# Where column sums, squares of x and one weight slot stand in a two-layer decoder kernel

## The chip, the cores and the metric

The kernel runs on one core of a Trainium2 chip. A core has a matrix engine (TensorE, PE in the profile; its weight loads are listed apart as PEld), a vector engine (VectorE, DVE), a scalar engine (ScalarE, ACT), a general engine (GpSimd, POOL) and an engine that only issues transfers (SyncE, SP). They share one on-chip memory of 128 partitions (SBUF); products land in a second one (PSUM) of eight banks, and transfers (DMA) bring data from main memory. Every engine works through its own list of instructions in order and waits for the others by semaphores. The metric is the device time of one execution in microseconds.

## What is computed

The reference is a decoder of two layers on 256 tokens of width 1024, each of which also attends into a fixed memory of 256 rows. Everything is float32. Cut to what matters here:

```
def _rmsnorm(x, g):
    y = x * lax.rsqrt(jnp.mean(x * x, axis=-1, keepdims=True) + EPS)
    return y * g

def _sq_relu_mlp(h, w_up, w_down):
    u = jax.nn.relu(h @ w_up)
    return (u * u) @ w_down

# layer A
h = _rmsnorm(x, a_norm_attn);  z = h @ a_w_in          # q, k, v, qm
...                                                    # rotation of q and k, differential attention
kv = _rmsnorm(mem, a_mem_norm) @ a_w_mem_kv            # keys and values of the memory
x = x + concat(o_self, o_mem) @ a_w_out
x = x + _sq_relu_mlp(_rmsnorm(x, a_norm_mlp), a_w_up, a_w_down)
# layer B: the same frame, block attention, with kv_norm, b_norm_attn, b_mem_norm, b_norm_mlp
# at the end: _rmsnorm(x, final_norm)
```

The norm's factor of a token, 1/sqrt(mean of squares), can be applied behind a product, since it scales whole rows. So the products run on `x * gain`, and the factor is needed only where a result leaves PSUM.

## The kernel before

**Products in three passes.** Every float32 operand is split in a high part (a rounded copy, `wh` for weights) and a low part (the rest, `wl`). A product is high times high, high times low and low times high. The weights come in 192 chunks of 128 x 1024 (512 KB each) into a ring `w` of four slots; ACT makes `wh` (line 354, a copy that rounds), DVE makes `wl` (line 356, a subtraction with two inputs), each into a ring of six slots. A slot is taken as the lowest free one when its first user is placed. `x` is kept transposed in `xT` (eight tiles of 128 x 256), and `x * gain` is split in the same way into `xn` (lines 370 and 372).

**Two places for xn.** `xn` lies in one room that is `LEAD` = 16 elements (64 bytes) longer than its content. The up stages read it from the room's start (`xnt`), the other stages 64 bytes further (`xnn`). The weights' slots all have one place within a line of 512 bytes, the same as that of `xnn`, by the order in which the tiles are laid out.

**A planner writes the order.** The program first lists its steps (`P.add`): engine, a duration in ns from a formula, what is read and written, and a priority, which is the step's number less a shift (`P.shift`). `Plan.order` then plays the steps through on its own clock: an engine that is free takes the ready step of the lowest priority whose buffers are free. The instructions of each engine are issued in the order that results. Transfers are steps of an engine `dma` whose durations are bytes over a rate: 390 bytes per ns for large ones, 290 for small ones, 310 for those of the start, and 1900 ns more until they land (3000 for `xnat`). A step of POOL and a step of DVE with two inputs are kept apart in time. No duration of the planner is measured when the kernel runs; if the chip is later than the plan, an engine waits at the instruction that the plan put next.

**Stages.** From 0 to about 124 us runs the attention of layer A (`mixer_a`), to 212 the up products of its MLP, to 282 the down products, to 410 the attention of layer B, to 500 the up products and to the end the down products of layer B. The first block of `mixer_a` (`qk_block`, products at lines 515 and 520) uses the first four weight chunks; its results leave PSUM scaled with x's factors (`ropes`, line 551), are rotated by POOL (line 562) and DVE (lines 568 and 570) and are turned by PE (line 586) for the first attention scores. There is one `ropes` buffer, so the two halves of the tokens follow each other. Then comes the product of the memory's rows (`mem_a`), whose tiles are made from `memt` by `mem_tiles`.

**Three ways to a norm's factor** (class `Stats`):
- `whole` loads the rows themselves (`xnat` or `mnat`, two transfers of 512 KB), squares and sums them along the row on ACT (line 456, four instructions) and ends with some twelve small DVE instructions (lines 461 to 464, with lines 412 to 421).
- `add` squares a tile of `xT` on ACT (line 473) and adds it to `sqa` on POOL (line 474).
- `rstd` sums `sqa` over the partitions with two one-column products on PE (line 483), which need a PSUM bank of the class `t`, and ends with the same chain on DVE, or with two instructions if only the square is wanted.

Layer A's first norm and the memory's norm use `whole`: `ra.whole(xnat, 2, 3000, pri=119.5)` and `mr.whole(mnat, 3)`.

**Up stages** (`mlp_up`). Sixteen steps `b` of two chunks each. A chunk is 16 products with `wh` and 8 with `wl`, all of 256 columns: a slice of weights is stationary and `xnt` moves (line 848). Between `b` = 4 and 11 the tiles of `xT` go through `add`; at `b` = 14 the column sum, `st.rstd(True)`, is listed, two steps (four chunks) ahead of the stage's end. Its result is used when the down stage's sums are scaled.

**Down stages** (`natural_down`, products of 512 columns at line 898) open four PSUM banks of the class `t`, and take part of the weights in pairs of chunks through `fast_pair`, where seven products replace eight.

Of the kernel before, what the change touches and what calls it, by code (L numbers as in the profile page):

```python
# [10 lines left out]
F32R = mybir.dt.float32r  # L11
# [6 lines left out]
D, S, FF = 1024, 256, 4096  # L18
KT = D // 128
# [6 lines left out]
FAST = (1, 3, 5, 7, 9, 11)  # L26
CW = 1024
LEAD = 16
WARM = 34


# [179 lines left out]
def t_act(n, psum=False, scale=False):  # L211
    return (51 if psum else 93) + 0.835 * n + (93 if scale else 0)


def t_dve(n, scalar=False):
    return 69 + 1.041 * n + (61 if scalar else 0)
# [11 lines left out]
def tile_hybrid(ctx: ExitStack, tc: tile.TileContext, x0, xa, xb, xc, memt, xnat, mnat, w0, wall, consts, fgain, out):  # L228
    nc = tc.nc
    const = ctx.enter_context(tc.tile_pool(name="const", bufs=1))  # L230
    ring = ctx.enter_context(tc.tile_pool(name="ring", bufs=1))
# [7 lines left out]
    P = Plan(caps, ("acc", "w", "wh", "wl", "v") + tuple(f"B{i}" for i in range(8)))  # L239
    uid = [0]  # L240

    def name(s):
        uid[0] += 1
        return f"{s}_{uid[0]}"

    def buf(cls, shape, dt=F32, pool=None):
        pool = pool or ring
        return Buf(cls, lambda slot: pool.tile(shape, dt, name=name(cls), tag=f"{cls}{slot}", bufs=1))
# [25 lines left out]
    NG = len(GAINS) * KT  # L274
    xg = fixed([128, NG + KT * S], "xT")
    xT = xg[:, NG:].rearrange("p (k s) -> p k s", k=KT)
    xroom = fixed([128, KT * 2 * S + LEAD], "xn", F32R)
    xnt, xnn = [xroom[:, a:a + KT * 2 * S].rearrange("p (k a s) -> p k a s", k=KT, a=2) for a in (0, LEAD)]
    g = {n: xg[:, i * KT:(i + 1) * KT] for i, n in enumerate(GAINS)}
# [18 lines left out]
    wu = psum.tile([128, 512], F32, name="wu", tag="t0", bufs=1)  # L298
    for _ in range(WARM):
        nc.tensor.matmul(wu[:, 0:128], ones_b, ones_b, start=True, stop=True)  # L300
# [22 lines left out]
        return deco  # L323

    def dma(dst, src, nbytes, r=(), w=(), pri=None, rate=0, lag=1900):
        rate = rate or (290 if nbytes <= 2100 * 128 else 390)
        P.add(("dma", max(470, nbytes / rate), lambda: nc.sync.dma_start(dst(), src)), r, w, lag=lag, pri=pri)  # L327


    st_ = {"i": 0, "pieces": 2, "layer": "A"}  # L330

    def chunk(dma_pieces=1, **a):
        i = st_["i"]
        st_["i"] += 1
        w = buf("w", [128, CW])
        h = buf("wh", [128, CW], F32R)
        l = buf("wl", [128, CW], F32R)
        hs = (0, 1)
        if dma_pieces == 1:
            dma(lambda: w.t, wall[i], 4 * 128 * CW, w=[(w, 0), (w, 1)], **a)  # L340
        else:
            for p in hs:
                dma(lambda p=p: w.t[:, p * 512:(p + 1) * 512], wall[i][:, p * 512:(p + 1) * 512] if i else w0[p],
                    256 * CW, w=[(w, p)], pri=(2 * i + 0.5 * p - 0.5) if i else 4 * p - 6, **a)
        old, P.shift = P.shift, EARLY["w" + st_["layer"]]
        for p in (hs if st_["pieces"] == 2 else [hs]):
            q = p if isinstance(p, tuple) else (p,)
            sl = slice(q[0] * 512, q[-1] * 512 + 512)
            n = 512 * len(q)
            if i == 0 and q[0] == 0:  # L350
                P.add(("dve", t_dve(n), lambda sl=sl: nc.vector.tensor_copy(h.t[:, sl], w.t[:, sl])),
                      [(w, x) for x in q], [(h, x) for x in q], pri=-9)
            else:
                P.add(("act", t_act(n), lambda sl=sl: nc.scalar.copy(h.t[:, sl], w.t[:, sl])),  # L354
                      [(w, x) for x in q], [(h, x) for x in q])
            P.add(("dve", t_dve(n), lambda sl=sl: nc.vector.tensor_sub(l.t[:, sl], w.t[:, sl],  # L356
                                                                       h.t[:, sl].bitcast(F32))),
                  [(w, x) for x in q] + [(h, x) for x in q], [(l, x) for x in q], port=True)
        P.shift = old
        return h, l  # L360
# [18 lines left out]
    def big(i, shape, dt=F32):  # L379
        return buf(f"B{i}", shape, dt)  # L380
# [12 lines left out]
    def mem_tiles(gname):  # L393

        hs, ls = [], []
        T = Tiles(lambda k: hs[k // 4].t[:, k % 4], lambda k: ls[k // 4].t[:, k % 4],
                  lambda k: (hs[k // 4], k % 4), lambda k: (ls[k // 4], k % 4))
        for a in range(2):
            w = buf("w", [128, 4, S])
            hs.append(buf("wh", [128, 4, S], F32R))  # L400
            ls.append(buf("wl", [128, 4, S], F32R))
            dma(lambda w=w: w.t, memt[:, 4 * a:4 * a + 4], 4 * 128 * CW, w=[w])
            for i in range(4):
                k = 4 * a + i
                early("mem")(split_scaled)(lambda w=w, i=i: w.t[:, i], [w], g[gname][:, k:k + 1], T, k)
        return T
# [396 lines left out]
    def mlp_up(st, sums=()):  # L803

        us = [big(i, [128, 4, 2, S], F32R) for i in range(8)]
        st_["pieces"] = 1
        for b in range(16):
            if 4 <= b < 12:
                st.add(lambda m=b - 4: xT[:, m], [("x", b - 4)])
            if b == 14:  # L810
                st.rstd(True)
            u = buf("u", [128, 2, S])
            ps = bank("acc")
            for mi in range(2):
                wh, wl = chunk()
                up_chunk(ps, mi, wh, wl)
            k0 = 2 * b % 4
            P.add(("act", t_act(512, True), lambda u=u, ps=ps: nc.scalar.activation(
                u.t, ps.t.rearrange("p (a s) -> p a s", a=2), AF.Relu)), [ps], [u])
            P.add(("act", t_act(512), lambda u=u: nc.scalar.activation(u.t, u.t, AF.Square)), [u], [u])  # L820
            if b in sums:
                dst, keys = sums[b]

                def blocks(u=u, dst=dst):
                    a = [u.t[:, k, hf * 128:hf * 128 + 128] for hf in range(2) for k in range(2)]
                    s = [dst()[:, i * 128:i * 128 + 128] for i in range(4)]
                    nc.vector.tensor_add(s[0], a[2], a[3])
                    nc.vector.tensor_sub(s[1], s[0], a[0])
                    nc.vector.tensor_sub(s[2], a[0], a[2])
                    nc.vector.tensor_sub(s[3], a[1], s[1])  # L830
                P.add(("dve", 4 * t_dve(128) + 100, blocks), [u], keys, port=True)
            P.add(("act", t_act(512), lambda u=u, t=us[b // 2], k0=k0: nc.scalar.copy(t.t[:, k0:k0 + 2, 0], u.t)),  # L832
                  [u], [(us[b // 2], b)])
            P.add(("dve", t_dve(512), lambda u=u, t=us[b // 2], k0=k0: nc.vector.tensor_sub(  # L834
                t.t[:, k0:k0 + 2, 1], u.t, t.t[:, k0:k0 + 2, 0].bitcast(F32))), [u, (us[b // 2], b)],
                [(us[b // 2], b, 1)], port=True)
        return us

    def ukeys(us, k):
# [38 lines left out]
    def natural_down(us, pss, upto, held, gather, room, rk, depth):  # L878
# [30 lines left out]
        def fast_pair(n, j):  # L909
# [2 lines left out]
            st_["i"] += 2  # L912
            w = [buf("w", [128, CW]) for _ in range(2)]
            h = [buf("wh", [128, CW], F32R) for _ in range(4)]
            l = [buf("wl", [128, CW], F32R) for _ in range(4)]
            for a in range(2):
                dma(lambda a=a: w[a].t, wall[i + a], 4 * 128 * CW, w=[(w[a], 0), (w[a], 1)])
            old, P.shift = P.shift, EARLY["w" + st_["layer"]]
# [227 lines left out]
    class Mixer:  # L1146


        def __init__(self, diff, rx, qT, kT):
            self.diff, self.rx, self.qT, self.kT = diff, rx, qT, kT  # L1150
            self.O = big_tiles(0, 1, 128 - LEAD)
            self.vv = big(4, [128, 4, 512]) if diff else None
# [145 lines left out]
    mr = Stats()  # L1298
# [14 lines left out]
    ra = Stats()  # L1313
    first_ch = []
    for k in range(KT):
        if k == 0:
            dma(lambda: xg[:, 0:NG + S], x0, 512 * (NG + S), w=["g", ("x", 0)], pri=-5, rate=310)
        if k == 1:
            dma(lambda: xg[:, NG + S:NG + 2 * S], xa, 512 * S, w=[("x", 1)], pri=-3, rate=310)
        if k == 2:  # L1320
            dma(lambda: xg[:, NG + 2 * S:NG + 4 * S], xb, 512 * 2 * S, w=[("x", 2), ("x", 3)], pri=-1, rate=310)
        if k in (4, 6):
            dma(lambda k=k: xg[:, NG + k * S:NG + (k + 2) * S], xc[k // 2 - 2], 512 * 2 * S,
                w=[("x", k), ("x", k + 1)], pri=k - 1, rate=310)
        if k % 2 == 0:
            first_ch.append(chunk(2, rate=310))
        split_scaled(lambda k=k: xT[:, k], [("x", k), "g"], g["a_norm_attn"][:, k:k + 1], xs_, k)
    ra.whole(xnat, 2, 3000, pri=119.5)
    dma(lambda: cst, consts, 512 * 513, w=["trig", "lam", "sub8"], pri=122)

    def lam_steps():
# [7 lines left out]
    ls, le = fixed([128, 2], "ls"), fixed([128, 2], "le")  # L1339
# [4 lines left out]
    def mem_a():  # L1344
        T = mem_tiles("a_mem_norm")
        pss = nat_block([(T, 0, 512)])
        mr.whole(mnat, 3)
        mem_evac(pss)

    ma = Stats()  # L1350
# [96 lines left out]
```

## Time and profile before

| | |
|---|---|
| time, three runs | 593.92 us median (592.78, 593.92, 595.08) |
| the profiled execution | 593.41 us, of which 590.5 are the span from its first to its last instruction |
| granted PE clock over the span | 0.997 |
| moved by DMA | 108.42 MB, mean 184 GB/s |

The time of the runs is taken around the whole program, the span inside the profile; between the two lie 2.9 us that no view resolves. In the groups of the profile a line such as L354 is the line of the code, followed by engine, operation and tiles (written <- read), the number of instructions, the time in which they kept the engine busy and the mean of one in ns. A matmul's duration there is longer than its pace, because products overlap in the array: the pace is read from starts, or from the length of a stretch over the number of products in it.

### The profile page before, as it was taken

To read this page: it belongs to the slowest core of one execution; us is meant where nothing else is said; L and a number is where in the kernel's file an instruction comes from. 1 tells how busy PE (TensorE), PEld (TensorE's weight loads), DVE (VectorE), ACT (ScalarE), POOL (GpSimd) and SP (SyncE) were. 2 spreads that over 40 slices of the span, in tenths; PEclk is the share of its full clock that TensorE was granted. 3 is DMA by queue.
4 is the path that set the end of the run, shared out by engine and by line. 5 is a ranking of instruction groups with operands and counts; after the bars stand their busy time and mean duration, and the time that the engine had idled before them with its cause. 6 is when DMAs were issued, how large, how long until landed. Compare 5 with 4: busy or idle time off the path is not lost.

```text
span 590.5 us, 10291 instructions
## 1 busy us (share of the span) xinstructions
PE 578.8 (98%) x3786; PEld 511.5 (87%) x3786; DVE 464.3 (79%) x816; ACT 408.1 (69%) x782; POOL 60.6 (10%) x67
## 2 busy tenths in 40 slices
PE   8989999999999999999999999999999999999995
PEld 6867778999999988888888887889999999888884
DVE  6668988877666689997988698796866667898785
ACT  6787888678677566557776588675876676665632
POOL 0023021242000000000112222000500000000002
PEclk9999999999999999999999999999999999999998
DMA  8965446337665536566476643425655564456531
GB/s 276 331 210 201 143 150 217 134 127 232 218 200 188 184 111 240 180 229 219 165 242 234 200 130 122 137 69 182 210 195 203 181 208 149 145 205 220 183 102 71
DMA packets 31153, 108.42 MB, mean 184 GB/s; under 512 B 3456, under 2 KB 3712, under 8 KB 31104
## 3 DMA queue, kind: packets, MB, share of 16 engines
q1 hardware_dynamic: 30816, 107.26, 53.9%
q8 instruction: 29, 0.48, 0.3%
q10 hardware_dynamic: 288, 0.52, 0.2%
q14 instruction: 20, 0.16, 0.1%
HBM read 106.72 MB, written 1.05 MB: 182 GB/s over the span
## 4 chain that ended last, share of the span: by engine, by line
PE 87%; DMA 4%; DVE 3%; ACT 3%; issue 1%; SPq 1%; POOL 0%; DVEq 0%; ACTq 0%
PE acc L848 30%; PE t L898 22%; PE acc L515 14%; PE acc L794 8%; PE acc L898 6%; DMA w<-wall 3%; PE t L615 2%; PE t L653 2%; PE t L710 1%; DVE wl L356 1%; DMA xT<-xc 1%; PE t L586 1%; SPq L327 1%; ACT B L634 0%; ACT B L456 0%
## 5 line engine op out<-in xcount | busy, mean ns | idle before, releaser
L356 DVE TENSOR_TENSOR wl<-w,wh 128x512 fp32r<-128x512 f32 (+1 forms) x232 | 213.8, 944 | 62.5 <-ACT wh L354 61.2
L354 ACT CAST wh<-w 128x512 fp32r<-128x512 f32 (+1 forms) x231 | 181.7, 818 | 117.4 <-PE acc L848 38.7
L848 PE MATMUL acc<-xn,wh 128*128 128x256 f32 x1024 | 128.5, 278 | 0.0
L848 PEld LDWEIGHTS acc<-xn,wh 128*128 128x128 f32 x1024 | 122.0, 188 | 0.3
L898 PE MATMUL t<-wh,B 128*128 128x512 f32 (+1 forms) x368 | 111.9, 386 | 0.0
L898 PEld LDWEIGHTS t<-wh,B 128*128 128x128 f32 x368 | 68.6, 188 | 13.7
L515 PE MATMUL acc<-wh,xn 128*128 128x512 f32 x220 | 72.8, 398 | 0.7 <-ACT wh L354 0.7
L898 PE MATMUL t<-wl,B 128*128 128x512 f32 (+1 forms) x184 | 71.0, 386 | 0.0
L848 PE MATMUL acc<-xn,wl 128*128 128x256 f32 x512 | 68.8, 277 | 0.0
L848 PEld LDWEIGHTS acc<-xn,wl 128*128 128x128 f32 x512 | 63.1, 188 | 0.0
L515 PEld LDWEIGHTS acc<-wh,xn 128*128 128x128 f32 x220 | 41.3, 188 | 11.3 <-ACT wh L354 1.5
L794 PE MATMUL acc<-B,wh 128*128 128x256 f32 x256 | 49.4, 286 | 0.0
L474 POOL TENSOR_TENSOR sqa<-sqa,sq 128x256 f32<-128x256 f32 x21 | 23.8, 1136 | 233.9 <-ACT sq L473 233.0
L515 PE MATMUL acc<-wl,xn 128*128 128x512 f32 x110 | 43.2, 393 | 0.5 <-DVE wl L356 0.5
L794 PEld LDWEIGHTS acc<-B,wh 128*128 128x128 f32 x256 | 40.4, 188 | 0.6 <-issue 0.5
L898 PEld LDWEIGHTS t<-wl,B 128*128 128x128 f32 x184 | 34.5, 188 | 7.1
L562 POOL TENSOR_TENSOR ropet<-ropes,consts 128x256 f32<-128x256 f32 (+1 forms) x28 | 26.6, 970 | 101.0 <-ACT ropes L551 84.0
L794 PE MATMUL acc<-B,wl 128*128 128x256 f32 x128 | 35.7, 279 | 0.0
L922 DVE TENSOR_TENSOR wl<-wsum,wh 128x1024 fp32r<-128x1024 f32 x24 | 29.2, 1222 | 2.2 <-ACT wh L921 1.5
L921 ACT CAST wh<-wsum 128x1024 fp32r<-128x1024 f32 x24 | 25.3, 1052 | 7.6 <-PE acc L848 3.6
L634 ACT ACTIVATE B<-t,small 128x128 f32<-128x128 f32 (+1 forms) x64 | 27.0, 437 | 4.2 <-DVE small L630 3.6
L834 DVE TENSOR_TENSOR B<-u,B 128x512 fp32r<-128x512 f32 x32 | 22.0, 689 | 9.9 <-ACT B L832 9.9
(227 smaller groups left out, 861.4 us busy)
## 6 DMA issues: line engine op xcount, KB each, us to landing
w<-wall SPq DMA_DIRECT2D x188, 512.0 KB, 4.0
w<-memt SPq DMA_DIRECT2D x4, 512.0 KB, 5.7
w<-wall SPq DMA_DIRECT2D x6, 256.0 KB, 5.2
B<-xnat SPq DMA_DIRECT2D x2, 512.0 KB, 8.8
B<-mnat SPq DMA_DIRECT2D x2, 512.0 KB, 7.9
w<-w SPq DMA_DIRECT2D x2, 256.0 KB, 3.4
xT<-xc SPq DMA_DIRECT2D x2, 256.0 KB, 5.8
consts<-consts SPq DMA_DIRECT2D x1, 256.5 KB, 8.3
```

The lines of the kernel that those rows point to most:

```text
L354: P.add(("act", t_act(n), lambda sl=sl: nc.scalar.copy(h.t[:, sl], w.t[:, sl])), [(w, x) for x in q], [(h, x) for x in q])
L356: P.add(("dve", t_dve(n), lambda sl=sl: nc.vector.tensor_sub(l.t[:, sl], w.t[:, sl], h.t[:, sl].bitcast(F32))), [(w, x) for x in q] + [(h, ...
L474: P.add(("pool", t_pool(S), lambda: nc.gpsimd.tensor_tensor(self.acc.t, self.acc.t, sq.t, op=OP.add)), [sq, self.acc], [self.acc])
L515: nc.tensor.matmul(pss[hf].t[:, c0:c1], a(k)[:, ts], b.t[:, o + c0:o + c1], start=(k == 0 and i == 0), stop=(k == KT - 1 and i == 2))
L562: nc.gpsimd.tensor_tensor(t.t[:, 0:nh, e:e + 32], zs.t[:, 0:nh, 32 - e:64 - e], b(sin[:, e:e + 32]), op=OP.mult)
L634: nc.scalar.activation(p[hd].t[:, c], sp[hd].t[:, c], AF.Exp, bias=nm[hd][:, qb:qb + 1], accum_out=ss[:, hd, qb:qb + 1])
L794: nc.tensor.matmul(o, a.t[:, ws], x(k), start=(n == 0 and m % 2 == 0 and i == 0), stop=(n == KT - 1 and i == 2), skip_group_check=True)
L834: P.add(("dve", t_dve(512), lambda u=u, t=us[b // 2], k0=k0: nc.vector.tensor_sub(t.t[:, k0:k0 + 2, 1], u.t, t.t[:, k0:k0 + 2, 0].bitcast( ...
L848: nc.tensor.matmul(ps.t[:, o], w.t[:, k * 128:(k + 1) * 128], xnt[:, k, x], skip_group_check=True, **flags)
L898: nc.tensor.matmul(ps.t[:, c0:c1], x, y, start=start and i == 0, stop=stop and i == 2, skip_group_check=True)
L921: P.add(("act", t_act(m), lambda: nc.scalar.copy(h[x].t[:, :m], src())), keys, [h[x]])
L922: P.add(("dve", t_dve(m), lambda: nc.vector.tensor_sub(l[x].t[:, :m], src(), h[x].t[:, :m].bitcast(F32))), keys + [h[x]], [l[x]], port=True)
```

## The change

It has five parts.

1. The low weights' slot 5 becomes 128 elements longer. In the up stages (`near=True`) the weights lie 112 elements from its start, elsewhere 128: 64 bytes lower in the up stages. The other five slots keep size and place within a line.
2. `st.rstd(True)` moves from `b` = 14 to behind the loop, so it is listed after the stage's last product.
3. `ra.whole(xnat, ...)` goes. Instead eight `ra.add` on the tiles of `xT` are listed, with a priority ten steps later than their number, and each also waits for the last low weights of the first block's fourth chunk (`first_ch[3][1]`, second half). `ra.rstd()` follows. The input `xnat` is no longer read.
4. `mr.whole(mnat, 3)` gets `after=[T.lk(7)]`: its two transfers wait for the low part of mem's last tile.
5. The planner's rate for transfers becomes 340 bytes per ns for all sizes.

```diff
+MN = 7
+SUMS = -10
...
-        rate = rate or (290 if nbytes <= 2100 * 128 else 390)
+        rate = rate or 340
...
+    def low_buf(shape=(128, CW), near=False):
+
+        def make(slot):
+            lead = (128 - LEAD * near) * (slot == 5)
+            t = ring.tile([128, CW + 128 * (slot == 5)], F32R, name=name("wl"), tag=f"wl{slot}", bufs=1)[:, lead:lead + CW]
+            return t if len(shape) == 2 else t.rearrange("p (k s) -> p k s", k=shape[1])
+        return Buf("wl", make)
+
-    def chunk(dma_pieces=1, **a):
+    def chunk(dma_pieces=1, near=False, **a):
...
-        l = buf("wl", [128, CW], F32R)
+        l = low_buf(near=near)
...
-            ls.append(buf("wl", [128, 4, S], F32R))
+            ls.append(low_buf((128, 4, S)))
...
-            if b == 14:
-                st.rstd(True)
...
-                wh, wl = chunk()
+                wh, wl = chunk(near=True)
...
+        st.rstd(True)
         return us
...
-            l = [buf("wl", [128, CW], F32R) for _ in range(4)]
+            l = [low_buf() for _ in range(4)]
...
-            dma(lambda: xg[:, 0:NG + S], x0, 512 * (NG + S), w=["g", ("x", 0)], pri=-5, rate=310)
+            dma(lambda: xg[:, 0:NG + S], x0, 512 * (NG + S), w=["g", ("x", 0)], pri=-5)
...
-            first_ch.append(chunk(2, rate=310))
+            first_ch.append(chunk(2))
...
-    ra.whole(xnat, 2, 3000, pri=119.5)
+    P.shift = SUMS
+    for k in range(KT):
+        ra.add(lambda k=k: xT[:, k], [("x", k), (first_ch[3][1], 1)])
+    ra.rstd()
+    P.shift = 0
...
-        mr.whole(mnat, 3)
+        mr.whole(mnat, 3, after=[T.lk(MN)])
```

The other transfers of the start lose their `rate=310` in the same way.

More of the change, by code (lines that the diff above doesn't have):

```diff
@@ L1316, in tile_hybrid @@
         if k == 0:
-            dma(lambda: xg[:, 0:NG + S], x0, 512 * (NG + S), w=["g", ("x", 0)], pri=-5, rate=310)
+            dma(lambda: xg[:, 0:NG + S], x0, 512 * (NG + S), w=["g", ("x", 0)], pri=-5)
         if k == 1:
-            dma(lambda: xg[:, NG + S:NG + 2 * S], xa, 512 * S, w=[("x", 1)], pri=-3, rate=310)
+            dma(lambda: xg[:, NG + S:NG + 2 * S], xa, 512 * S, w=[("x", 1)], pri=-3)
         if k == 2:
-            dma(lambda: xg[:, NG + 2 * S:NG + 4 * S], xb, 512 * 2 * S, w=[("x", 2), ("x", 3)], pri=-1, rate=310)
+            dma(lambda: xg[:, NG + 2 * S:NG + 4 * S], xb, 512 * 2 * S, w=[("x", 2), ("x", 3)], pri=-1)
         if k in (4, 6):
             dma(lambda k=k: xg[:, NG + k * S:NG + (k + 2) * S], xc[k // 2 - 2], 512 * 2 * S,
-                w=[("x", k), ("x", k + 1)], pri=k - 1, rate=310)
+                w=[("x", k), ("x", k + 1)], pri=k - 1)
         if k % 2 == 0:
-            first_ch.append(chunk(2, rate=310))
+            first_ch.append(chunk(2))
         split_scaled(lambda k=k: xT[:, k], [("x", k), "g"], g["a_norm_attn"][:, k:k + 1], xs_, k)
-    ra.whole(xnat, 2, 3000, pri=119.5)
+    P.shift = SUMS
[3 more added lines that the diff above has]
+    P.shift = 0
     dma(lambda: cst, consts, 512 * 513, w=["trig", "lam", "sub8"], pri=122)
```

## The prediction

> **What bounds the kernel now.** I read the busy shares first, then busy time by stage, then the chain of waits where a stage has a hole.
>
> ```profile
> PE 578.8 (98%) x3786; PEld 511.5 (87%) x3786; DVE 464.3 (79%) x816; ACT 408.1 (69%) x782; POOL 60.6 (10%) x67
> ...
> w<-wall SPq DMA_DIRECT2D x188, 512.0 KB, 4.0
> B<-xnat SPq DMA_DIRECT2D x2, 512.0 KB, 8.8
> B<-mnat SPq DMA_DIRECT2D x2, 512.0 KB, 7.9
> ```
>
> ```profile
> 10.00:39.00 29.00, 29.00 (x129) 23.73 (x128) 19.53 (x46) 21.80 (x51) 1.94 (x2) 1.00 0.91 324
> 39.00:44.00 5.00, 2.67 (x15) 1.68 (x13) 4.24 (x8) 5.00 (x13) 2.09 (x2) 1.00 0.12 21
> 44.00:124.00 80.00, 79.61 (x547) 67.17 (x547) 68.07 (x173) 63.16 (x184) 13.95 (x14) 1.00 0.51 170
> ```
>
> The columns of the stages are length, then busy PE, PEld, DVE, ACT, POOL, then granted clock, DMA share, GB/s. PE is busy everywhere except in 39 to 44 us, where it works 2.67 of 5.00 us at a full clock. From 10 to 39 the DMA engines are 91% busy. So time can be won in two ways: close that hole, or make PE's own products follow each other faster. PE in the hole, then the chain behind it:
>
> ```profile
> 39.64 0.27 PE L586 MATMUL t<-ident,B 128*128 128x128 f32 x1
> 42.06 0.98 PE L586 MATMUL t<-ident,B 128*128 128x128 f32 x7 [2.15 <-DVE B L570]
> 42.80 0.48 PE L515 MATMUL acc<-wh,wh 128*128 128x512 f32 x1
> 43.46 0.50 PE L515 MATMUL acc<-wl,wh 128*128 128x512 f32 x1 [0.17 <-DVE wl L356]
> ...
> 44.22 0.38 PE L608 MATMUL t<-mask_b,ident_b 128*128 128x128 bf16 x4
> ```
>
> ```profile
> 14.40 8.73 DMA w<-wall
> ...
> 25.21 6.25 DMA w<-wall
> ...
> 32.62 0.74 ACT ropes L551 x2
> 33.36 2.30 ACT B L456 x7
> ...
> 38.39 0.73 ACT ropes L551 x2
> ...
> 39.19 2.10 POOL ropet L562 x2
> ...
> 41.32 0.04 DVE B L570
> ```
>
> Seven transposes take 42.80-42.06 = 0.74 us, so the stretch 39.64 to 42.06 holds 0.1 us of work and 2.3 of waiting. The next three products take 1.42 us where three take 0.68 at full pace (twice the 113.3 ns that 256 columns take in the up stages, below): another 0.7, some 0.1 of it a restart. The hole is worth **2.9 us**. The chain says why: two weight loads that took 8.73 and 6.25 us where the median is 4.0, since they shared the queue with the whole-row copies of x and mem (`xnat`, `mnat`), and then ACT, which squares `mnat` (L456, 2.30 us) between the first rope and the second.
>
> **The change part by part.** First the **up stages**. In each, the column sum stands four chunks (96 products) ahead of the end:
>
> ```profile
> 200.33 0.50 PE L483 MATMUL t<-ones,sqa 128*128 128x1 f32 x4
> 200.69 2.13 PE L848 MATMUL acc<-xn,wh 128*128 128x256 f32 x16
> ...
> 203.60 2.05 PE L848 MATMUL acc<-xn,wh 128*128 128x256 f32 x16
> ```
>
> ```profile
> 189.45:200.33 10.88, 10.88 (x98) 1.00 0.59 191
> 200.69:212.08 11.39, 11.39 (x96) 1.00 0.56 186
> 477.74:488.62 10.88, 10.88 (x98) 1.00 0.56 191
> 488.98:500.37 11.39, 11.39 (x96) 1.00 0.53 181
> ```
>
> The four rows are the 96 products before the sum and the 96 after it, in both stages. 10.88/96 is 113.3 ns a product, 11.39/96 is 118.6: after the interruption PE goes on at a slower pace and doesn't recover by the end of the stage. Of the 0.51 us, about 0.09 is the restart itself (the first sixteen take 2.13, the next sixteen 2.05) and goes with the sum wherever it stands; **0.42 per stage, 0.84 in all**, is the pace. Behind the last product come products of 512 columns; the first and the last of a run that begins 0.70 us into them:
>
> ```profile
> 212.78 0.62 PE L898 MATMUL t<-wh,B 128*128 128x512 f32 x2
> ...
> 225.48 0.39 PE L898 MATMUL t<-wl,B 128*128 128x512 f32 x1
> ```
>
> 56 products in 12.70 us are 226.8 ns each, the full pace: there the slow one ends by itself within three products. The sum's result is used at the end of the down stage; its `t` bank is one of four that the down stage opens one after the other, 0.68 us apart, so I cost that at nothing; without this cover it is the sum's two short DVE steps, 0.4 us.
>
> **Slot five**: 64 bytes lower in the up stages alone. Does the place of a low weight matter today? Six chunks in a row go through the six slots, by the code's rule of taking the lowest free one, and each takes the same time; the first and last of six equal rows:
>
> ```profile
> 184.01:186.73 2.72, 2.72 (x27) 2.72 (x25) 1.00 0.52 185
> ...
> 197.61:200.33 2.72, 2.72 (x26) 2.68 (x24) 1.00 0.53 185
> ```
>
> So there is nothing to win at full pace: 0. A gain is bounded by what slow pace may be left at a stage's head: 0.11 us a chunk (11.30 less 10.88 over four), 0.2 over two chunks. The other end: no row has a 256-column product whose stationary and moving tiles stand on the same 64-byte place of a 512-byte line, which the shift makes of this slot (low weights otherwise stand 64 bytes above `xn`'s). The nearest row of trouble is the same slow pace; for the slot's own eight products that is 0.04 a chunk, 0.4 over some 11 chunks; if PE then stays slow as it does behind the sum, much more (rival 3). I take 0, the row of equal chunks.
>
> **Squares of x from its tiles.** Removed: two loads of 512 KB at 13 to 16 us, four 512-wide squares on ACT. Added: eight 256-wide squares on ACT, seven adds on POOL, a column sum on PE, the same chain on DVE less one step.
>
> ```profile
> 15.14 1.14 ACT L354 CAST wh<-w 128x512 fp32r<-128x512 f32 x2 [1.58 <-PE acc L515]
> 18.18 1.14 ACT L354 CAST wh<-w 128x512 fp32r<-128x512 f32 x2 [1.89 <-DMA w<-wall]
> ```
>
> ```profile
> L473 ACT ACTIVATE sq<-xT x21: 400/404/424, 123.8 to 422.2; 128x256 f32<-128x256 f32 x21
> ```
>
> ```profile
> L474 POOL TENSOR_TENSOR sqa<-sqa,sq x21: 737/998/1977, 124.2 to 424.0; 128x256 f32<-128x256 f32 x21
> ```
>
> ```profile
> 13.08 1.29 DVE L356 TENSOR_TENSOR wl<-w,wh 128x512 fp32r<-128x512 f32 x2
> ...
> 25.81 0.16 DVE L461 TENSOR_TENSOR small<-small 128x2 f32<-128x2 f32 x1 [0.63 <-ACT B L456]
> ...
> 27.99 0.17 DVE L464 TENSOR_SCALAR small<-small 128x2 f32<-128x2 f32 x1
> ```
>
> The squares may begin when the first block's last low weights are written, 14.4 us. Eight times 0.404 is 3.2 us of ACT, beside its idle 1.58+1.89 = 3.5; without that cover the second block's weights would be late by up to 3.2. POOL, which works 1.94 us in all of 10 to 39, needs 7 x 0.998 = 7.0: done by about 22.2. The sum costs PE 200.69-200.33 = 0.36, a restart of 0.09, 0.45 in all, and this **adds 0.45**. The DVE chain takes 28.16-25.81 = 2.35, so x's factors stand at 25 to 26.5 instead of 28.2. In PE's queue the sum blocks what is behind it if POOL is later than the planner thinks: it counts 677 ns an add (t_pool(256)) and lets DVE's two-input steps and POOL wait for each other, so uncontended the error is 737-677 = 60 ns an add, 0.4 us in seven; at the median it is 2.2. I take **0.4**, nearest to the uncontended row since contention is in the plan, and keep 0 and 2.2.
>
> ```profile
> 127.49 7.84 POOL L474 TENSOR_TENSOR sqa<-sqa,sq 128x256 f32<-128x256 f32 x5 [2.51 <-ACT sq L473]
> ```
>
> Here five adds beside the low-weight subtractions took 1.57 us each. The Trainium skill, page "SBUF — State Buffer", section "Who interferes with whom", says that a VectorE instruction with two SBUF inputs and a GpSimd one that reads SBUF exclude each other for a whole instruction, the later one blocking; this row agrees with it. By that rule alone, without the plan's allowance, it speaks against this part: it is rival 1.
>
> **mem's rows later, loads re-rated.** `mnat` now waits for the last low tile of mem; the loads' durations in the planner go to one rate, which changes orders and no instruction.
>
> ```profile
> 52.48 0.48 DVE L372 SCALAR_TENSOR_TENSOR wl<-w,xT,wh 128x256 fp32r<-128x256 f32 x1
> ```
>
> ```profile
> 73.47 0.47 ACT L539 ACTIVATE mk<-acc,small 128x256 f32<-128x256 f32 x1 [0.33 <-DVE small L421]
> ```
>
> That tile is ready at 52.95. Add 7.9 for the landing, 0.8 for the second load, 2.3 for squares, 2.4 for DVE: 66.4, ahead of the 73.47 where its factors are first used. SP waits there with the weight loads behind it, which then share the queue with 1 MB; I cost that at nothing, as the hole that DMA kept open is gone by then, and at up to 1.5 us (half of 1 MB at 324 GB/s) if PE runs dry. Re-ordering elsewhere has only the 0.39 us of idle PE in 44 to 124 to win, and as its other end one more hole of 2.3.
>
> What goes from the chain to 41.3: 4.7 and 2.2 us of late landings and ACT's 2.3. Less than 2.9 of it is needed. With the factors at 26.5 the two ropes take what they took (41.4-32.6 = 8.8) less 2.3: 33 us, long before PE asks at 39.64. Late next are the mem product's weights (L356 at 43.46), behind the same ACT queue. I take all of the 2.3 and half of the 0.6: **-2.6**.
>
> Sum: -2.6 +0.45 +0.4 -0.84 = -2.6. The profiled execution took 593.41 us (its span and 2.9 around it), 0.5 under the median of 593.92; -2.6 gives 590.8 for it and **591.3** on the median's scale. 0.5% is 3.0 us, about what a measurement of this kernel can tell from no change.
>
> **The rivals.** (1) The wait is replaced: PE stands at the column sum while POOL, blocked by DVE, finishes. For it speaks 1.57 us an add, against it the plan's allowance. Seven adds then end at 14.8+11.0 = 25.8, 3.6 later than 22.2; the plan expects a part of that, so I price PE's loss at the 2.2 of the median add instead of 0.4: 593.1. (2) The hole stays: the second rope is held by POOL and DVE order, or the mem tiles are late, and only the pace is won: -0.84+0.45 = -0.4, 593.5. For it: ACT is busy 5.00 of 5.00 us there. Against it: 2.3 of ACT's work before it goes. (3) Slower: slot five puts PE onto the slow pace, which then lasts. Price 0.11 us a chunk; from the first such chunk 26 of 32 are behind it in each stage, 52 x 0.11 = 5.7: 597.0. It decides from 25 slow chunks on, where it eats the 2.6. For it: PE kept the slow pace for 96 products twice. Against: the slot never showed a difference. (4) More goes: the rest of the hole, no wait at the sum and the 0.39 us: 589.6. (5) The sums don't end up behind the last product, because the planner orders by its own clock: 592.1.
>
> **How the numbers follow.** Forecast 0.47, (1) 0.15, (2) 0.14, (3) 0.10, (4) 0.10, (5) 0.04. The forecast's own range is 590.2 to 592.3. The whole range leaves out (3) and the tail of (1): 589.0 to 595.0, where the upper end holds the 2.2 us wait on top of an open hole (593.5+1.8) nearly whole. Faster by over 0.5% means below 590.95: (4) and six tenths of the forecast's mass, 0.38. Slower by over it means above 596.9: (3) and little else, 0.12. Within: 0.50.
>
> **What would show it.** PE busy in 39 to 44 near 5.00; no `xnat` load; first weight landings of the second block near 4 us; POOL's seven adds done before PE reaches L483; each chunk of an up stage at 2.72 to its end, slot five's too; L483 right ahead of the first L898. I am wrong if PE waits at L483 on POOL for over 1 us, if a new hole of over 1 us opens before 80 us, or if chunks take 2.83 outside a stage's head.

## The result, and the profile after

| | before | after |
|---|---|---|
| median | 594.08 us (592.78 to 595.08) | 597.31 us (596.28 to 598.16) |
| profiled execution | 593.41 us, span 590.5 | 596.28 us, span 594.1 |

The ratio is 1.0062, with a 95% interval of 1.0038 to 1.0085: slower by 0.6%, where 591.3 was forecast and 595.0 was the upper end of the range. Rival 3 stood at 597.0.

Line numbers have moved: products of the up stages L848 to L857, of the down stages L898 to L907, of the first block L515 to L525, column sums L483 to L493, squares L473 to L483, their adds L474 to L484.

The page after, busy shares and the issues of transfers:

```profile
PE 585.1 (98%) x3790; PEld 517.8 (87%) x3790; DVE 468.1 (79%) x816; ACT 407.9 (69%) x781; POOL 66.1 (11%) x74
...
w<-wall SPq DMA_DIRECT2D x188, 512.0 KB, 3.8
...
B<-mnat SPq DMA_DIRECT2D x2, 512.0 KB, 7.1
```

The load of `xnat` is gone. PE has four matrix products more (the two of the new column sum, which the profile lists as four) and is busy for 6.3 us longer (585.1 against 578.8). So the loss isn't waiting: the same products take longer. Where, the busy time by stage shows; after first, then the same stages before:

```profile
10.00:39.00 29.00, 28.45 (x128) 23.25 (x127) 24.92 (x50) 20.14 (x44) 9.59 (x11) 1.00 0.73 253
39.00:44.00 5.00, 4.80 (x33) 3.48 (x31) 3.71 (x7) 4.80 (x12) 1.15 (x2) 1.00 0.63 208
44.00:122.01 78.01, 77.95 (x530) 65.51 (x529) 67.39 (x169) 63.11 (x187) 12.71 (x13) 1.00 0.53 176
122.01:212.57 90.56, 90.56 (x770) 90.28 (x769) 62.23 (x90) 63.16 (x91) 9.02 (x7) 1.00 0.56 187
212.57:411.27 198.70, 198.70 (x1117) 166.24 (x1116) 167.35 (x297) 137.63 (x279) 19.51 (x23) 1.00 0.53 175
411.27:503.29 92.02, 92.02 (x786) 91.91 (x785) 63.71 (x90) 65.58 (x95) 8.66 (x7) 1.00 0.57 189
503.29:594.10 90.81, 83.89 (x390) 69.95 (x388) 72.84 (x107) 47.31 (x67) 5.03 (x7) 0.97 0.43 151
```

```profile
123.69:212.08 88.39, 88.39 (x774) 88.15 (x773) 63.22 (x91) 62.78 (x91) 9.13 (x7) 1.00 0.59 191
212.08:410.35 198.27, 198.27 (x1113) 165.81 (x1111) 167.13 (x295) 137.69 (x279) 19.36 (x23) 1.00 0.52 176
410.35:500.37 90.02, 90.02 (x790) 89.92 (x789) 64.00 (x92) 64.89 (x95) 8.63 (x7) 1.00 0.58 193
500.37:590.50 90.13, 83.40 (x386) 69.52 (x384) 72.89 (x105) 47.31 (x67) 5.04 (x7) 0.98 0.43 152
```

The start did what was forecast: PE works 4.80 us of the 5 where it worked 2.67, and the first up stage begins 1.68 us earlier (122.01 against 123.69). The up stages then lose it: +2.17 and +2.00 us, though their column sum of 0.36 us now lies behind them. The stretches behind them take 0.43 and 0.68 us more, of which 0.36 each is that sum. -1.68 +2.17 +0.43 +2.00 +0.68 = 3.60 us, the difference of the spans. The granted clock is 1.00 in every one of these stages but the last, which has 0.97 (0.98 before).

PE at the first chunk of slot five, in order of time (start, busy us, instructions). Consecutive starts, divided by the count, give the pace:

```profile
130.40 1.07 PE L857 MATMUL acc<-xn,wl 128*128 128x256 f32 x8
131.31 1.98 PE L857 MATMUL acc<-xn,wh 128*128 128x256 f32 x16
133.12 1.12 PE L857 MATMUL acc<-xn,wl 128*128 128x256 f32 x8
134.08 1.34 PE L857 MATMUL acc<-xn,wh 128*128 128x256 f32 x10
...
136.20 2.05 PE L857 MATMUL acc<-xn,wh 128*128 128x256 f32 x16
138.08 1.10 PE L857 MATMUL acc<-xn,wl 128*128 128x256 f32 x8
```

Up to 133.12 the pace is the fast one: (133.12-131.31)/16 = 113 ns. The eight low products of slot five take (134.08-133.12)/8 = 120 ns. Behind them, with ordinary slots, sixteen take (138.08-136.20)/16 = 117.5 ns. No wait stands in these rows. The same line over longer windows, in both up stages:

```profile
136.20:153.17 16.97, 16.97 (x146) 16.97 (x145) 1.00 0.67 224
...
195.60:212.57 16.97, 16.97 (x146) 16.93 (x144) 1.00 0.54 183
424.25:426.97 2.72, 2.72 (x26) 2.72 (x25) 1.00 0.60 196
...
429.74:503.29 73.55, 73.55 (x626) 73.50 (x624) 1.00 0.56 187
```

The first two windows hold six chunks (144 products) each, right behind the slot and at the stage's end: 117.8 ns both times. The third is the last chunk before slot five in the second stage, 2.72 us or 113.3 ns a product; the fourth the 26 chunks behind it, 73.55/26 = 2.83 us each. (The number after x counts a product that overlaps a window's edge in both.) So PE falls from the fast pace to the slow one at the slot's first chunk and stays there: 27.75 chunks of the first stage and 26 of the second, each 0.11 us longer, are 5.9 us.

### The profile page after: what moved, and what is told of

It is laid out like the page before. It is cut to its first block, busy times and chain, and to the rows that moved or that the text cites. A ratio compares the mean times of both kernels' runs of the same rounds, so it can differ in the third digit from the quotient of the medians.

```text
span 594.1 us, 10310 instructions
## 1 busy us (share of the span) xinstructions
PE 585.1 (98%) x3790; PEld 517.8 (87%) x3790; DVE 468.1 (79%) x816; ACT 407.9 (69%) x781; POOL 66.1 (11%) x74
## 4 chain that ended last, share of the span: by engine, by line
PE 86%; ACT 4%; DMA 4%; DVE 3%; issue 1%; SPq 1%; POOL 0%; DVEq 0%; ACTq 0%; POOLq 0%
PE acc L857 30%; PE t L907 22%; PE acc L525 13%; PE acc L804 7%; PE acc L907 6%; DMA w<-wall 2%; PE t L625 2%; PE t L663 1%; ACT wh L364 1%; PE t L720 1%; DVE wl L366 1%; DMA xT<-xc 1%; DMA w<-memt 1%; ACT B L644 1%; PE t L525 1%
## 5 line engine op out<-in xcount | busy, mean ns | idle before, releaser
L366 DVE TENSOR_TENSOR wl<-w,wh 128x512 fp32r<-128x512 f32 (+1 forms) x232 | 216.5, 955 | 63.1 <-ACT wh L364 61.8
L364 ACT CAST wh<-w 128x512 fp32r<-128x512 f32 (+1 forms) x231 | 181.7, 818 | 117.5 <-PE acc L857 39.4
L857 PE MATMUL acc<-xn,wh 128*128 128x256 f32 x1024 | 131.6, 281 | 0.0
L857 PEld LDWEIGHTS acc<-xn,wh 128*128 128x128 f32 x1024 | 125.2, 189 | 0.4 <-DVE xn L382 0.2
L907 PE MATMUL t<-wh,B 128*128 128x512 f32 (+1 forms) x368 | 112.1, 386 | 0.0
L907 PEld LDWEIGHTS t<-wh,B 128*128 128x128 f32 x368 | 68.5, 188 | 13.7
L525 PE MATMUL acc<-wh,xn 128*128 128x512 f32 x220 | 72.8, 398 | 0.0
L907 PE MATMUL t<-wl,B 128*128 128x512 f32 (+1 forms) x184 | 71.0, 386 | 0.0
L857 PE MATMUL acc<-xn,wl 128*128 128x256 f32 x512 | 70.6, 281 | 0.0
L857 PEld LDWEIGHTS acc<-xn,wl 128*128 128x128 f32 x512 | 64.7, 189 | 0.0
L484 POOL TENSOR_TENSOR sqa<-sqa,sq 128x256 f32<-128x256 f32 x28 | 29.7, 1062 | 253.5 <-ACT sq L483 251.3
L525 PEld LDWEIGHTS acc<-wh,xn 128*128 128x128 f32 x220 | 41.3, 188 | 10.1 <-issue 1.4
L525 PE MATMUL acc<-wl,xn 128*128 128x512 f32 x110 | 43.1, 392 | 0.2 <-DVE wl L366 0.2
L907 PEld LDWEIGHTS t<-wl,B 128*128 128x128 f32 x184 | 34.5, 188 | 7.1 <-DVE wl L366 0.2
```

The lines of the kernel that those rows point to most:

```text
L484: P.add(("pool", t_pool(S), lambda: nc.gpsimd.tensor_tensor(self.acc.t, self.acc.t, sq.t, op=OP.add)), [sq, self.acc], [self.acc])
L525: nc.tensor.matmul(pss[hf].t[:, c0:c1], a(k)[:, ts], b.t[:, o + c0:o + c1], start=(k == 0 and i == 0), stop=(k == KT - 1 and i == 2))
L857: nc.tensor.matmul(ps.t[:, o], w.t[:, k * 128:(k + 1) * 128], xnt[:, k, x], skip_group_check=True, **flags)
L907: nc.tensor.matmul(ps.t[:, c0:c1], x, y, start=start and i == 0, stop=stop and i == 2, skip_group_check=True)
```

## The experiments

Theory one, from these rows: the shift of slot five costs all of it, because it puts these weights on `xnt`'s place, and PE keeps the pace that this sets. In the built programs the distance from `xnt` to every weight slot is 64 bytes (modulo 512), and 0 to slot five after the change. Theory two: the moved column sums or the new order of the planner bring the slow pace. In each diff only the core is shown, and the quoted text behind it is what was expected before the run. Ratios are to the kernel before, run beside each kernel on the same chip.

### Undo the shift, and make it alone

`e1_no_shift` is the kernel after with the shift taken out:

```diff
-                wh, wl = chunk(near=True)
+                wh, wl = chunk()
```

> The changed kernel with slot 5 at the same place in the up stages as elsewhere (its tile stays longer, so every other tile stays where it was). Theory A, the shift puts PE on the slow pace: chunks at 2.72 us from the stage's head to its end, the 5.6 us of slow pace gone but for 0.2 to 0.4 at the heads, 591.5 to 592.3 us. Theory B, the slow pace comes from the new order or the new layout and not from the shift: chunks stay at 2.83, 597 us.

`e2_shift_alone` is the kernel before with `low_buf` and nothing else of the change:

```diff
-                wh, wl = chunk()
+                wh, wl = chunk(near=True)
```

> The kernel before with the slot's shift as the only change. Theory A: from the first chunk of slot 5 on, chunks take 2.83 us in both up stages; the four chunks behind each column sum were slow already, so about 44 chunks times 0.11 is 4.8 us, and 0.2 more for the slot's own products at 120 ns: 599 us. Theory B: no change, 594 us.

Measured: e2 598.27 us (596.31 to 599.08), ratio 1.0069 (1.0044 to 1.0094); e1 593.33 us (589.84 to 595.53), ratio 0.9989 (0.9963 to 1.0014). The shift alone is as slow as the whole change, so the cause is the shift, and theory two falls. In e2's second stage, around the column sum at 493.43:

```profile
490.60:493.43 2.83, 2.83 (x26) 2.78 (x24) 1.00 0.51 177
495.69:496.60 0.91, 0.91 (x10) 0.91 (x9) 1.00 0.12 41
496.60:499.37 2.77, 2.77 (x26) 2.77 (x25) 1.00 0.68 220
499.37:502.20 2.83, 2.83 (x27) 2.83 (x25) 1.00 0.51 164
```

A slow chunk ahead of the sum, then eight products in 0.91 us (113.8 ns, fast) behind it, then slot five (2.77) and slow again. The sum that turns a fast PE slow (before: 10.88 us for four chunks ahead of it, 11.39 behind) turns a slow PE fast.

But e1 isn't at 591.3, where the forecast without the shift stood, nor within its own expectation of 591.5 to 592.3, and its executions spread over 5.7 us. Its profile says why; the two up stages and one chunk of each:

```profile
123.44:214.26 90.82, 90.82 (x768) 90.51 (x768) 1.00 0.56 186
412.98:502.13 89.15, 87.89 (x768) 87.39 (x768) 1.00 0.59 196
148.31:151.13 2.82, 2.82 (x26) 2.82 (x25) 1.00 0.98 369
449.54:452.26 2.72, 2.72 (x26) 2.72 (x25) 1.00 0.53 194
```

The first stage is slow from its first chunk to its last with no slot shifted and no sum in it; the second is fast throughout. A stage may start at either pace, and without an interruption it keeps it.

### Sums back, x's rows back

`e3_sum_back` is e1 with the column sums at `b` = 14 again; `e4_x_rows` is e1 with `ra.whole(xnat, 2, 3000, pri=119.5)` in place of the squares of tiles:

```diff
+            if b == 14:
+                st.rstd(True)
...
-        st.rstd(True)
```

> No shift, and the column sum of the up stages back at step 14. If moving it saves the pace of four chunks in each stage: 0.84 us longer than without the shift alone, chunks at 2.83 behind the sum. Rival, the move only carries the loss into the down stage: no difference between the two.

> No shift, and x's factors from its rows again (two loads of 512 KB, four squares) in place of the squares of its tiles. If the squares of tiles are what closed the hole at 39 to 44 us: about 1.5 us longer than without the shift alone, and the hole is back in part. Rival, that mem's later rows and the new rates closed it: no difference, or up to 1.1 us shorter, as PE then has no column sum there (0.45) and no wait for POOL (0.55).

Measured: e3 591.51 us (589.76 to 593.91), ratio 0.9958 (0.9935 to 0.9980); e4 592.14 us (590.44 to 595.31), ratio 0.9975 (0.9950 to 1.0000). The four chunks ahead of e3's first sum and the four behind it:

```profile
187.81:198.69 10.88, 10.88 (x98) 10.85 (x96) 1.00 0.56 193
199.06:210.45 11.39, 11.39 (x96) 11.34 (x96) 1.00 0.55 181
```

The 0.51 us of the prediction is there to the hundredth. Where a stage is fast, moving the sum out wins about that: e1's second stage takes 89.15 us, e3's takes 78.27+0.36+11.39 = 90.02, of which 0.36 is the sum. Yet in the median e1 is 1.8 us above e3, which neither theory expected. A stage that starts slow costs up to 32 x 0.11 = 3.5 us; a sum at `b` = 14 could end that for the last four chunks alone, 0.4 us, so the sum's place doesn't explain the difference. More slow starts in e1's executions than in e3's would: in the profiles the first stage is slow in e1 and fast in e3, though both have the same instructions up to e3's sum. That this is what e1's spread consists of is not shown for each execution. e4's times fall into two clusters (590.4 to 591.4 and 594.1 to 595.3, with one at 592.9 between), and its profiled execution has a slow first stage too; it can't tell the two ways to x's factor apart, which is taken up again below.

### Every weight on the place, and slot five elsewhere

`e5_xn_on_place` takes the shift out and moves `xnt` instead, so that all weights stand at distance 0 in the up stages; `e6_other_way` moves slot five up instead of down (distance 128); `e7_half` moves it by half (distance 32); `e8_first_only` shifts it as in the change, in the first four steps alone:

```diff
# e5, on e1
-    xnt, xnn = [... for a in (0, LEAD)]
+    xnt, xnn = [... for a in (LEAD, LEAD)]
# e6; its slot is 144 longer instead of 128, so some tiles behind it move by 64 bytes
-            lead = (128 - LEAD * near) * (slot == 5)
+            lead = (128 + LEAD * near) * (slot == 5)
# e7
-            lead = (128 - LEAD * near) * (slot == 5)
+            lead = (128 - 8 * near) * (slot == 5)
# e8
-                wh, wl = chunk(near=True)
+                wh, wl = chunk(near=b < 4)
```

> No shift of slot 5, but the up stages read xn 64 bytes further on, so that every stationary tile and the moving tile start at the same place of a 512-byte line. Theory A, a product whose two tiles share that place is itself slow (120 ns) and leaves PE slow: every chunk takes 24 x 120 = 2.88 us, both stages 92.2 us long, 10 us over the best times of the kernel without the shift, about 600 us. Theory B, what matters is that one slot differs from the others: all chunks at one pace of 2.72 or 2.83, 590 to 595 us.

> The changed kernel with slot 5 shifted 64 bytes up instead of down in the up stages: its place is neither xn's nor that of the other weights. Theory A (shared place): slot 5's products at 113 or 118 ns like their neighbours, no chunk turns from fast to slow, 590 to 595 us. Theory B (a slot that differs): slot 5's products at 120 ns and everything behind them slow, 597 us.

> The changed kernel with slot 5 shifted by 32 bytes down instead of 64, half way to xn's place. Theory A with a grain of 64 bytes: as without the shift, 590 to 595 us. Theory A with a grain of 32 or less than that, or theory B: slow behind slot 5, 597 us.

> The changed kernel with the shift in the first eight chunks of each up stage alone, which hold one chunk of slot 5 per stage. If the slow pace lasts once it is entered: all chunks behind that one at 2.83, nearly the whole loss, 596 to 597 us. If each chunk of slot 5 slows only its neighbours: back to 2.72 within six chunks, 591 to 592 us.

| kernel | distance of slot five | median (range) | ratio to before (95%) |
|---|---|---|---|
| e5 | 0, and all others 0 | 600.97 us (600.40 to 601.63) | 1.0095 (1.0060 to 1.0130) |
| e6 | 128 | 592.40 us (591.21 to 594.08) | 0.9953 (0.9913 to 0.9993) |
| e7 | 32 | 591.58 us (590.24 to 593.15) | 0.9948 (0.9912 to 0.9984) |
| e8 | 0 in four steps, then 64 | 596.53 us (595.71 to 597.78) | 1.0031 (0.9991 to 1.0070) |

One chunk at the start and one near the end of e5's first up stage; six chunks behind the only shifted one in e8's first stage and the last six of that stage; in e7, slot five's eight low products and the four chunks behind them:

```profile
136.96:139.84 2.88, 2.88 (x27) 2.88 (x26) 1.00 0.40 141
203.19:206.07 2.88, 2.88 (x26) 2.88 (x25) 1.00 0.58 195
```

```profile
136.56:153.52 16.96, 16.96 (x147) 16.96 (x145) 1.00 0.68 223
195.92:212.88 16.96, 16.96 (x146) 16.91 (x144) 1.00 0.57 186
```

```profile
133.28:134.22 0.94, 0.94 (x10) 0.94 (x9) 1.00 0.13 52
136.26:147.14 10.88, 10.88 (x98) 10.88 (x97) 1.00 0.61 195
```

In e5 every chunk takes 2.88 us, 120.0 ns a product: that is the price of distance 0 itself. e8 has one such chunk in a stage, and 16.96/144 = 117.8 ns from there to the end: the pace lasts without its cause. In e7 the slot's own products take 0.94/8 = 117.5 ns, and the four chunks behind it 10.88/96 = 113.3: a distance of 32 slows the slot and leaves nothing behind. e6 reads the same (0.95 for the eight, then 10.88).

The Trainium skill, page "TensorE: Matmul & The Clock Gate", section "Step-by-step: what each phase is for", says that PE reads the moving and the stationary operand through two independent ports, so that loading the next weights takes no read bandwidth from the running product; page "SBUF — State Buffer", section "Who interferes with whom", says that PE never waits on anyone. By these sentences alone the place of the weights would not matter; in these rows it does: the same instructions at a clock of 1.00 take 113.3, 117.8 or 120.0 ns, by the place of one operand, by what went before and, at a stage's start, by the execution. The measurement decides; what in the chip makes it no row here shows.

### How far apart the bad places lie

`e11_scan` gives slots 2 to 5 distances of 192, 256, 320 and 448 bytes in the up stages; slots 0 and 1 stay at 64:

```diff
-            lead = (128 - LEAD * near) * (slot == 5)
+            lead = {2: 32, 3: 48, 4: 64, 5: 96}.get(slot, 0) * near
```

> No slot on xn's place; in the up stages the slots 2, 3, 4 and 5 stand 192, 256, 320 and 448 bytes above xn's place in a 512-byte line, slots 0 and 1 and all high weights 64 bytes as before. Known so far: 0 bytes 120 ns and slow behind it, 32 and 128 bytes 118 ns and fast behind it, 64 bytes 113 or 118 ns, whichever PE was at. If only the same place matters: all four at 113 or 118 like their neighbours, none at 120. If the distance sets a product's own pace: each slot has its own number in every one of its chunks, and one of them may be 113 with a fast neighbour behind it always. About 592 us either way.

Measured: 596.61 us (595.98 to 598.13), ratio 1.0031 (1.0009 to 1.0054). The low products of the first four chunks, by distance 192, 320, 256 and 448, then the next low products at 256:

```profile
127.93:128.84 0.91, 0.91 (x11) 0.91 (x9) 1.00 0.00 0
130.65:131.56 0.91, 0.91 (x11) 0.91 (x9) 1.00 0.95 369
132.01:132.97 0.96, 0.96 (x11) 0.96 (x9) 1.00 0.86 282
134.85:135.79 0.94, 0.94 (x10) 0.94 (x9) 1.00 0.36 126
...
148.28:149.23 0.95, 0.95 (x10) 0.95 (x9) 1.00 0.92 246
```

Eight fast products take 0.91 us, slow ones 0.94, those at 256 bytes 0.95 to 0.96. 192 and 320 leave PE fast; 256 does what 0 does; 448, met on the slow pace, leaves it slow. So among the distances tried the bad place comes back after 256 bytes. The time is some 4.6 us over what was expected, because one of the four slots stood on a bad place.

### Does the half shift end the slow pace, or only not start it?

Both up stages of e7's profile began fast. `g12_trip_and_mend` shifts by the full 64 bytes in the first four steps and by 32 in the rest:

```diff
-                wh, wl = chunk(near=True)
+                wh, wl = chunk(near=LEAD if b < 4 else LEAD // 2)
```

Here `near` is the shift itself (`lead = (128 - near) * (slot == 5)`).

> In the first four steps of each up stage slot five stands 64 bytes lower, on xnt's place, and in the later steps 32 bytes lower. As with the kernel that shifts in the first four steps alone, one chunk of each stage stands on xnt's place. Theory one, the distance of 32 bytes brings PE back from the slow pace to the fast one: about six chunks of each stage at 2.83 us, those between the two chunks of slot five, the rest at 2.72; up stages 87.65+0.7 and 89.24+0.7; 591.6+1.3 = 592.9 us. Theory two, that distance only doesn't start the slow pace, but doesn't end it either: slow from the first chunk of slot five to the end, up stages near 90.4 and 91.9 as in that kernel, 596.5 us.

Measured: 593.7 us (593.32 to 594.67), ratio 0.9996 (0.9965 to 1.0027), between the two theories. Two chunks ahead of slot five in the second stage, then four behind its chunk at distance 0, five behind its first chunk at 32, four behind its second:

```profile
422.25:427.69 5.44, 5.44 (x50) 5.44 (x49) 1.00 0.79 255
428.65:439.96 11.31, 11.31 (x99) 11.31 (x97) 1.00 0.61 190
447.50:461.63 14.13, 14.13 (x122) 14.13 (x121) 1.00 0.54 185
465.31:476.19 10.88, 10.88 (x98) 10.88 (x97) 1.00 0.59 193
```

2.72 a chunk, then 2.83, still 2.83 behind the first chunk at 32 bytes, and 2.72 behind the second. The first stage, which also began slow, shows the same: slow behind its first chunk at 32 bytes, fast behind its second. So the half shift does bring PE back, but not at each chance. Theory one holds with that correction; why the first chunk fails stays open. It also fits e7's narrow range: a stage that starts slow doesn't stay so.

### The start, on top of the half shift

With the pace steadied, three kernels on e7 each undo one part: `f4_x_rows` loads x's rows again, `f9_mem_rows_early` drops the wait of mem's rows, `f10_rates` puts back the planner's old rates:

```diff
# f4, in place of the eight ra.add and ra.rstd()
+    ra.whole(xnat, 2, 3000, pri=119.5)
# f9
-        mr.whole(mnat, 3, after=[T.lk(MN)])
+        mr.whole(mnat, 3)
# f10, with rate=310 at the start's loads again
-        rate = rate or 340
+        rate = rate or (290 if nbytes <= 2100 * 128 else 390)
```

> The 32-byte shift, which let PE be fast behind slot 5, with x's factors from its rows again. If the squares of tiles closed the hole at 39 to 44 us: the up stage begins 1 us or more later than at 122.1, and 1 to 1.5 us more than 591.6. Rival, the later rows of mem or the rates did: the same time or up to 1 us less.

> The 32-byte shift, with mem's rows loaded early again, ahead of mem's tiles. If their transfers and the four squares on ACT held the hole open: 1 to 2 us more than 591.6 and a hole of 1 to 2 us near 40 us. Rival, with x's rows gone there is room for them: no difference.

> The 32-byte shift, with the planner's rates of before (310 at the start, 290 and 390 behind). If the rates only re-order and win nothing: 591.6 within 0.6. Rival, they shortened the first 10 us, where PE was busy 8.72 us instead of 7.71: 0.7 to 1 us more.

Measured: f4 591.86 us, ratio 0.9965 (0.9948 to 0.9982); f9 591.94 us, 0.9961 (0.9945 to 0.9978); f10 592.76 us, 0.9986 (0.9970 to 1.0001). PE in 39 to 44 us, for e7, f4, f9 and f10:

```profile
39.00:44.00 5.00, 4.91 (x33) 3.68 (x31) 4.45 (x8) 4.90 (x12) 1.05 (x2) 1.00 0.58 188
```

```profile
39.00:44.00 5.00, 4.74 (x31) 3.35 (x30) 3.80 (x10) 4.24 (x10) 1.40 (x2) 1.00 0.46 142
```

```profile
39.00:44.00 5.00, 4.91 (x32) 3.59 (x31) 4.68 (x8) 4.64 (x12) 2.15 (x3) 1.00 0.35 112
```

```profile
39.00:44.00 5.00, 4.30 (x30) 2.94 (x28) 3.14 (x6) 5.00 (x13) 1.05 (x2) 1.00 0.68 227
```

Between 39 and 44 us the hole of 2.3 us stays shut when either the rows of x or the early rows of mem come back; no run put back both, so which of the removed transfers and squares closed it stays open. Part of the wait moves: in f4's profile PE stands 1.06 us at 61 us and 0.91 us at 80 us, where e7's longest wait after 44 us is 0.14. The old rates leave 0.6 us of the hole open (5.00-4.30 against 0.09 in e7); their whole cost, 592.76 against 591.9 for f4 and f9, is near 1 us, with intervals that overlap. The reason given for it, a shorter start, isn't borne out: of the first 10 us PE works 7.99 in f10 and 7.55 in e7. e7 ran in an earlier round, beside a kernel before at 595.20 us instead of 594.18, so differences under 1 us from it can't be read.

## Why the prediction was wrong

**The step that failed is "Slot five": "There is nothing to win at full pace: 0 ... I take 0, the row of equal chunks".** That row showed six slots at one and the same distance from `xnt`; it couldn't speak of a slot at another. The prediction said that no row has a 256-column product with both tiles on the same place, and then took the value of a row that didn't cover the case. The profile before does have such products. Near the end of the last down stage stand 36 of 256 columns, whose moving weights lie at distance 0 from the stationary `B` in the built program:

```profile
579.65 0.40 PE L898 MATMUL t<-wh,B 128*128 128x256 f32 x2
...
583.25 0.40 PE L898 MATMUL acc<-wh,B 128*128 128x256 f32 x2
```

From one start to the other there are 30 products in 3.60 us, 120.0 ns each, just what slot five's products then took. So the price of the place was there to be read; that the slow pace lasts behind it was not. The products of 512 columns with `B` lie at distance 0 too, and the prediction's own row has them at 226.8 ns, the full pace: the place told in these products of 256 columns and not in those of 512. The other end stood in rival 3, "PE onto the slow pace, which then lasts", at 52 chunks x 0.11 = 5.7 us; the profile after has 53.75 such chunks and 5.9 us. Mechanism and size of the rival were right, and a chance of 0.10 was too small for what the rows allowed. The argument against it, "the slot never showed a difference", was no evidence: nothing had moved the slot before.

**The start** was right in its time. The stage begins 1.68 us earlier, -2.6 +0.45 +0.4 = -1.75 was forecast. PE at the new column sum, then the adds of POOL that it waited for:

```profile
23.87 0.61 PE L493 MATMUL t<-ones,sqa 128*128 128x1 f32 x4 [0.55 <-POOL sqa L484]
```

```profile
L484 POOL TENSOR_TENSOR sqa<-sqa,sq x7: 728/845/1067, 14.0 to 23.1; 128x256 f32<-128x256 f32 x7
```

The wait was 0.55 us where 0.4 was taken; the adds' median of 845 ns lies between the row without contention and the median that gave the upper end. Rival 1 didn't come. Of the signs named, one came in part: the late weight load (8.73 us at 14.40) still takes 5.92 us at 14.14, not near 4. That the sum agrees to 0.07 is partly luck: the profiles of e1 and e3, which have the same instructions up to the first up stage, begin it at 123.44 and 122.06.

**Sums behind the last product** went where the prediction had them, so rival 5 is out:

```profile
211.63 1.10 PE L857 MATMUL acc<-xn,wl 128*128 128x256 f32 x8
212.57 0.50 PE L493 MATMUL t<-ones,sqa 128*128 128x1 f32 x4
212.93 0.70 PE L907 MATMUL t<-wh,B 128*128 128x512 f32 x2
```

Their -0.84 rested on one profiled execution with both stages fast. The rows were read rightly (e3 repeats them), the step from them to every execution was wrong: a stage can start slow, and then the sum inside it helps, by up to 0.4 us. In the kernel after nothing was left to win, since both stages were slow already.

**mem's rows and the rates**, costed at nothing: right for the rows within what f9 can tell, and for the rates perhaps 1 us too careful.

**Slips in the working** that change nothing above: rival 4's terms, 0.3+0.4+0.39, give 590.2 and not 589.6. Rival 1 lets the adds begin at 14.8 us, the main estimate at 22.2-7.0 = 15.2. And PE was not busy everywhere but in the hole: it worked 7.71 of the first 10 us.

Without the failed step the time comes out near the forecast: e7, which differs from the kernel after in 32 bytes of one slot, takes 591.58 us where 591.3 was forecast. It is faster than both kernels, by 0.5% (0.2 to 0.9) against the one before. That it agrees to 0.3 us is partly luck, since the kernel before took 595.20 us beside it, not 593.92.

## What to carry to other kernels

Where one operand's place is moved, compare its distance to the operand that is read beside it, modulo 256 bytes as far as these runs go, and don't cost it from rows in which all distances are equal. In a long run of equal matrix products read the pace by consecutive starts at several points of the stretch: a step in it that persists is a state, not a wait, and one chunk can set it. And before a small gain is taken from one profiled execution, see whether other executions ran at the same pace.

## What the runs showed of the hardware beyond that

- A product of 256 float32 columns has three paces at a granted clock of 1.00: 113.3, 117.8 and 120.0 ns. The first two are kept over whole stages (768 products) with identical addresses and instructions; which of them a stage starts with differs between stages (e1: 90.82 us for the slow stage; 89.15 for the fast one, which holds more work of other kinds) and between executions (e1 and e3). In the profiles here the first stage of e1, e4 and g12 began slow, and no second stage did.
- For these products, distance 0 or 256 bytes between stationary and moving tile: 120 ns, and slow behind. At 512 columns distance 0 shows no loss (226.8 ns a product). 32 or 128: about 118 ns for its own products, fast behind where PE came from fast, and from slow at 32 bytes at the second chance. 64, 192 and 320 leave the fast pace as it is, and 64, 192, 320 and 448 the slow one.
- A column sum of 0.36 us in the middle of such products changes the pace in either direction: fast to slow in before and e3, slow to fast in e2.
